# Mixer of a residual block on one core: small transfers begun a hook ahead, one attention score per step, attention's vector and scalar work at the evacuations' priority

## The chip, the cores and the metric

The kernel runs on one core of a Trainium2 chip. The metric is the device time of one execution in microseconds (us), the median of several runs. TensorE (PE) multiplies, VectorE (DVE) and ScalarE (ACT) do elementwise work, GpSimd (POOL) a little, SyncE (SP) issues the transfers.

## The reference

One layer over a sequence of 512 tokens with 2048 features: a normalised and modulated input goes through one projection, whose columns feed a gated linear recurrence (RG-LRU) and eight heads of attention with a forget gate; both are normalised, projected back and added. Then a SwiGLU feed-forward block. Cut to the part in question:

```python
mod = c_act @ w_ada[l] + b_ada[l]
sh1, sc1, gt1, sh2, sc2, gt2 = jnp.split(mod, 6, axis=-1)
h = modulate(rms_norm(x, g_mix[l]), sh1, sc1)
xr, yr, q, k, v, f_logit = jnp.split(h @ w_in[l], splits, axis=-1)
# recurrence: u = conv(xr); r, i = gates of u; a = exp(-8 r softplus(-lam))
#   h_t = a h_(t-1) + sqrt(1 - a^2) (i u);  y_rec = h * gelu(yr)
# attention, per head and block of 128 queries:
s = jnp.einsum('bhqd,bhkd->bhqk', qb, kb)
s = s + cum[:, :, q0:q1, None] - cum[:, :, None, :q1]
p = jax.nn.softmax(jnp.where(mask, s, -jnp.inf), axis=-1)
outs.append(jnp.einsum('bhqk,bhkd->bhqd', p, vb))
# x = x + gt1 * (concat(rms(y_rec), rms(y_att)) @ w_out), then the SwiGLU block
```

## The kernel before, in words

Activations lie with features on the 128 partitions and the 512 tokens along the row. Every fp32 product is three matmuls of a high and a low part (names ending in h and l), so each weight tile is transferred raw, copied to its high part by ScalarE (L187) and its low part taken by VectorE (L188). The order of the stages is: the recurrence's input columns, the first half of the gate columns, head h0, heads h1 to h7, the second half of the gate columns, then output projection, up and down projections.

A head group (`tm_group`) makes q, k and v of one head: 384 columns, 16 steps of 12 matmuls (L192), one step for each 128 input features. Work of other kinds hangs on steps as hooks: while h4's matmuls run, attention of head 3 is done, and so on. `ATT_STEPS` gives the steps after which the parts of `attention` come: statistics of q and k (L463 to L467), transposes qkt into `qkT` (L474, L476), the bias `bt` from the cumulated forget gate (L486), four scores `s` (L494) each reduced to a row minimum `nm` together with the bias (L498, in the rows CUSTOM_DVE or ISA), exponential (L500), reciprocal and scaling (L501, L502), transposes `pt` of the probabilities (L508) copied to `pT` (L511), and the products `po` with v (L519). The scores and `pt` use three PSUM buffers between them ("misc").

In h1 and h2 the sums of bias (the shift sh1 through the weights) are made: 48 transfers of 128x512 into `bw` (two buffers, L564, L565) and as many additions into `ba` (L568, L570); in h3 `binp` sums `ba` over the partitions on TensorE (L575). From h3 on, `rec_pair` does two recurrence columns per head: it loads `xrl` (L585), scales and convolves it (L587 to L592), loads gate weights `gw` (L596), makes gates on TensorE (L602) and their functions (L609 to L620, square roots L625), scans (L629) and multiplies with the gelu of `yrl` (L636 to L652). `REC_STEPS` says where its first parts stand, `CARRY` where the rest stands in the next head. Blocks of the modulation (`ada`: a transfer of 512 KB in two halves, L136, and two 128x1024 multiplications on VectorE, L139) fill up at the steps `H_ADA`.

A scheduler puts each engine's instructions into one list, by priority and by when their operands are there, and each engine runs its list in order. Evacuations of PSUM and what the next head needs stand at offset 2500 (`EVAC`), weight transfers and splits at 2000 (`AHEAD`), attention's and the recurrence's other work at the normal one, ada below it at -300 (`ADA_LATE`).

Of the kernel before, what the change touches and what calls it, by code (L numbers as in the profile page):

```python
# [44 lines left out]
YR0_AHEAD = 80  # L45
CARRY = (0, 0, 1, 1, 1, 3, 6)
WO_ADA = 5
# [15 lines left out]
def block_kernel(ctx, tc, xT, crow, adaT, vecs, bfr, w1, wyr, wqkv0, wqkv, wgate, wout, wup0, wups, wdown, outT):  # L63
# [67 lines left out]
    mods = [cp.tile([P, KT], F32, name=f"mod{j}") for j in range(6)]  # L131

    def ada_block(j, i):
        for hf in range(2):
            t = ap_.tile([P, 1024], F32, tag="ada", name=f"ada{j}_{i}_{hf}")
            nc.sync.dma_start(out=t, in_=adaT[j * KT + i, :, hf * 1024:(hf + 1) * 1024])  # L136
# [22 lines left out]

    def ada_some(n):  # L160
        with tc.high_priority(offset=ADA_LATE), tc.issue_after(tail_lo[-1]):
            for _ in range(n):
                if pending:
                    pending.pop(0)()

    def queue_ada(j, fin=None):
        for i in range(KT):
            pending.append(lambda j=j, i=i: ada_block(j, i))
        last = pending.pop()

# [240 lines left out]
    def forget(ps):  # L411
        z = cp.tile([P, NT * NH], F32, name="z")
        z3 = z.rearrange("p (t h) -> p t h", t=NT)
        for t in range(NT):
            nc.vector.tensor_add(z3[:, t, :], ps[t][:, 384:392], bfb)

        def rest():
            lf = cp.tile([P, NT * NH], F32, name="lf")
            log1p_exp(lf, z, NT * NH, "lf")
            nc.vector.scalar_tensor_tensor(out=lf, in0=z, scalar=0.0, in1=lf, op0=ALU.min, op1=ALU.subtract)  # L420
            pc = rgp("pc")
            nc.tensor.matmul(pc[:, 0:32], lhsT=triu, rhs=lf, start=True, stop=True)
# [16 lines left out]
        return rest  # L439

# [15 lines left out]
    def attention(h, q, k, v):  # L456
# [12 lines left out]
        def qk_t():  # L469
            qkT = []  # L470
            for a, z, g in ((0, q, gqs), (1, k, vcol(V_GK))):
# [3 lines left out]
                zt = page(f"qkT{h}_{a}", "b")  # L475
                nc.scalar.activation(zt, pt, AF.Copy, scale=g)  # L476
                qkT.append(zt)
# [11 lines left out]
        def score(b):  # L489
# [7 lines left out]
            nm, sm = small(1, f"nm{h}_{b}"), small(1, f"sm{h}_{b}")  # L497
            nc.vector.tensor_tensor_reduce(out=p[:, :n], in0=ps[:, :n], in1=p[:, :n], scale=-1.0, scalar=3.0e38,  # L498
                                           op0=ALU.add, op1=ALU.min, accum_out=nm)
            nc.scalar.activation(p[:, :n], p[:, :n], AF.Exp, scale=-1.0, bias=nm, accum_out=sm)  # L500
            nc.vector.reciprocal(sm, sm)  # L501
            nc.vector.tensor_scalar_mul(p[:, :n], p[:, :n], sm)  # L502

        def pt_(kb):
# [5 lines left out]
            pT = page(f"pT{h}_{kb}", "b")  # L510
            nc.scalar.activation(pT[:, qs], pt[:, qs], AF.Copy)  # L511
            st[kb] = pT
# [44 lines left out]
    ba = []  # L557

    def bias_in(kt):
        if kt == 0:  # L560
            ba.extend(page(f"ba{j}", "c") for j in range(3))
        for j, sd in enumerate((w1[kt][:, :512], w1[kt][:, 512:],
                                wyr[0][kt // 4][:, (kt % 4) * 512:(kt % 4 + 1) * 512])):
            src = ap_.tile([P, S], F32, tag="x", name=f"bw{kt}_{j}", bufs=2)  # L564
            nc.sync.dma_start(out=src, in_=sd)  # L565
            s1 = sh1[kt]
# [12 lines left out]
    def rec_pair(ns):  # L579
        X, U, GP, RG, IG, last = {}, {}, {}, {}, {}, {}  # L580
        PG = []

        def conv(n):
            x = page(f"xrl{n}", "c")
            nc.sync.dma_start(out=x, in_=xr[n])  # L585
            X[n] = x
            nc.vector.tensor_mul(x, x, rstd_x)  # L587
# [6 lines left out]
            U[n] = u  # L594
            gw = page(f"gw{n}", "c", [P, 256])
            nc.sync.dma_start(out=gw, in_=wgate[n])  # L596
            GP[n] = gw

# [23 lines left out]
        def scan():  # L622
# [5 lines left out]
            for n in ns:  # L628
                nc.vector.tensor_tensor_scan(out=U[n], data0=RG[n], data1=IG[n], initial=0.0, op0=ALU.mult, op1=ALU.add)  # L629
                hs[n] = U[n]  # L630

        def finish():
            for n in ns:
                if n < 4:
                    yl = page(f"yrl{n}", "c")
                    nc.sync.dma_start(out=yl, in_=yr[n])  # L636
                    nc.scalar.activation(yl, yl, AF.Identity, bias=bin_[:, 8 + n:9 + n])
# [31 lines left out]
    for h in range(NH):  # L669
# [413 lines left out]
```

## Time and profile before

| | |
|---|---|
| median of 3 runs | 2160.18 us (2156.42 to 2160.85) |
| the profiled execution | 2160.95 us, span 2158.9 us |
| PE busy | 2099.0 us (97%) |
| DVE busy | 1532.5 us (71%) |
| ACT busy | 859.0 us (40%) |
| mean granted clock of TensorE | 0.992 |
| the chain that ended last | PE 82%, DVE 8%, DMA 6% |

The profiled execution is 2.05 us longer than its span, the time before the first and after the last instruction. The head groups lie between 149 and 536 us; from 186 us on h1 runs. The shares above are over the whole span; the windows below split it.

### The profile page before, as it was taken

The numbers are of one execution on the slowest core, as the hardware profiler recorded it, in microseconds if no ns is written. First come the engines' busy times: TensorE is split into PE (matmuls) and PEld (weight loads), VectorE is DVE, ScalarE is ACT, GpSimd is POOL, SyncE is SP. The second block draws the span as 40 slices with busy tenths as digits, with TensorE's granted clock in tenths as the row PEclk, the third lists the DMA queues.
The fourth block names the chain that finished last, engine by engine and source line by source line (L and its number), as shares of the span: only waits on it lengthen the run. The fifth ranks groups of instructions, "written<-read, shape, count | busy, mean of one in ns | idle before, by whom it ended". The sixth has DMA issues, their size and how long they took to land.

```text
span 2158.9 us, 32248 instructions
## 1 busy us (share of the span) xinstructions
PE 2099.0 (97%) x12737; PEld 1904.1 (88%) x12737; DVE 1532.5 (71%) x2407; ACT 859.0 (40%) x1200; POOL 32.9 (2%) x37
## 2 busy tenths in 40 slices
PE   8998988989999999999999999999999999999999
PEld 6788887878878887999999999999999888888887
DVE  8997668887787689988888888888887443323332
ACT  4433336765443245544444444444444222221111
POOL 0000000000010000000000000000000000000000
PEclk9999999999999999999999999999999999999999
DMA  9987666666768742434334344344345985553442
GB/s 336 349 299 253 200 210 225 203 211 230 245 222 286 260 142 79 146 127 141 124 128 142 123 128 141 123 128 147 118 130 178 335 294 175 204 195 136 154 154 102
DMA packets 133016, 406.00 MB, mean 188 GB/s; under 512 B 14561, under 2 KB 19841, under 8 KB 123138
## 3 DMA queue, kind: packets, MB, share of 16 engines
q1 hardware_dynamic: 132866, 403.96, 55.4%
q8 instruction: 99, 1.62, 0.3%
q14 instruction: 51, 0.42, 0.1%
HBM read 361.15 MB, written 42.75 MB: 187 GB/s over the span
## 4 chain that ended last, share of the span: by engine, by line
PE 82%; DVE 8%; DMA 6%; issue 2%; ACT 1%; POOL 1%; SPq 0%; DVEq 0%; ACTq 0%
PE dn_0p L192 6%; PE dn_3p L192 6%; PE dn_2p L192 6%; PE dn_1p L192 6%; PE w1p L192 4%; PE yr1p L192 2%; PE up0p L192 2%; PE wo3p L192 2%; PE wo2p L192 2%; PE wo1p L192 2%; PE up1p L192 2%; PE yr0p L192 2%; DMA bw<-in_w 2%; DMA ada<-in_adaT 2%; PE wo0p L192 2%
## 5 line engine op out<-in xcount | busy, mean ns | idle before, releaser
L139 DVE SCALAR_TENSOR_TENSOR ada<-ada,c_b 128x1024 f32<-128x1024 f32 x128 | 154.7, 1219 | 50.0 <-DMA ada<-in_adaT 49.9
L188 DVE TENSOR_TENSOR uq_0tl<-uq_0r,uq_0th 128x1024 fp32r<-128x1024 f32 x40 | 49.0, 1225 | 62.0 <-ACT uq_0th L187 62.0
L187 ACT ACTIVATE uq_0sh<-uq_0r 128x1024 fp32r<-128x1024 f32 x40 | 42.5, 1062 | 90.6 <-PE uf6p L955 2.3
L188 DVE TENSOR_TENSOR uq_0al<-uq_0r,uq_0ah 128x1024 fp32r<-128x1024 f32 x40 | 49.0, 1225 | 39.2 <-ACT uq_0ah L187 39.1
L187 ACT ACTIVATE uq_1sh<-uq_1rb 128x1024 fp32r<-128x1024 f32 x40 | 42.5, 1063 | 70.6 <-PE uf43p L955 2.4
L187 ACT ACTIVATE uq_0th<-uq_0r 128x1024 fp32r<-128x1024 f32 x40 | 42.4, 1060 | 70.9 <-PE uf30p L955 2.1
L187 ACT ACTIVATE uq_1th<-uq_1ra 128x1024 fp32r<-128x1024 f32 x40 | 42.4, 1061 | 70.3 <-DVE uq_1sl L188 1.8
L187 ACT ACTIVATE uq_1ah<-uq_1ra 128x1024 fp32r<-128x1024 f32 x40 | 42.4, 1061 | 60.0 <-issue 58.5
L187 ACT ACTIVATE uq_0ah<-uq_0r 128x1024 fp32r<-128x1024 f32 x40 | 42.4, 1060 | 49.3 <-issue 45.5
L188 DVE TENSOR_TENSOR uq_1tl<-uq_1ra,uq_1th 128x1024 fp32r<-128x1024 f32 x40 | 49.0, 1225 | 10.0 <-ACT uq_1th L187 9.8
L570 DVE SCALAR_TENSOR_TENSOR ba<-bw,sh,ba 128x512 f32<-128x512 f32 x45 | 33.3, 749 | 27.7 <-DMA bw<-in_w 14.7
L192 PE MATMUL w1p<-hph,w1h 128*128 128x512 f32 x128 | 47.1, 396 | 6.0 <-ACT hph L333 6.0
L188 DVE TENSOR_TENSOR uq_0sl<-uq_0r,uq_0sh 128x1024 fp32r<-128x1024 f32 x40 | 49.0, 1226 | 3.7
L188 DVE TENSOR_TENSOR uq_1sl<-uq_1rb,uq_1sh 128x1024 fp32r<-128x1024 f32 x40 | 49.0, 1226 | 3.2 <-ACT uq_1sh L187 0.9
L192 PE MATMUL w1p<-hpl,w1h 128*128 128x512 f32 x128 | 50.6, 396 | 0.0
L192 PE MATMUL w1p<-hph,w1l 128*128 128x512 f32 x128 | 50.3, 393 | 0.0
L188 DVE TENSOR_TENSOR uq_1al<-uq_1ra,uq_1ah 128x1024 fp32r<-128x1024 f32 x40 | 48.6, 1214 | 0.0
L149 DVE SCALAR_TENSOR_TENSOR ada<-ada,c_b 128x1024 f32<-128x1024 f32 x32 | 38.9, 1217 | 2.4 <-DMA ada<-in_adaT 2.4
L188 DVE TENSOR_TENSOR dn_1l<-dn_2r,dn_1h 128x1024 fp32r<-128x1024 f32 x11 | 13.5, 1226 | 38.0 <-ACT dn_1h L187 38.0
L188 DVE TENSOR_TENSOR dn_0l<-dn_2r,dn_0h 128x1024 fp32r<-128x1024 f32 x11 | 13.5, 1225 | 37.6 <-ACT dn_0h L187 37.6
L188 DVE TENSOR_TENSOR dn_1l<-dn_0r,dn_1h 128x1024 fp32r<-128x1024 f32 x11 | 13.5, 1225 | 37.4 <-ACT dn_1h L187 37.4
L188 DVE TENSOR_TENSOR dn_0l<-dn_0r,dn_0h 128x1024 fp32r<-128x1024 f32 x11 | 13.5, 1226 | 37.0 <-ACT dn_0h L187 37.0
(13787 smaller groups left out, 8171.1 us busy)
## 6 DMA issues: line engine op xcount, KB each, us to landing
ada<-in_adaT SPq DMA_DIRECT2D x160, 512.0 KB, 5.5
uq_0r<-in_wups SPq DMA_DIRECT2D x80, 512.0 KB, 4.1
uq_1ra<-in_wups SPq DMA_DIRECT2D x40, 512.0 KB, 4.0
uq_1rb<-in_wups SPq DMA_DIRECT2D x40, 512.0 KB, 3.2
adf<-in_adaT SPq DMA_DIRECT2D x32, 512.0 KB, 5.9
actd<-ach SPq DMA_DIRECT2D x44, 256.0 KB, 2.0
actd<-acl SPq DMA_DIRECT2D x44, 256.0 KB, 4.0
dn_0r<-in_wdown SPq DMA_DIRECT2D x11, 1024.0 KB, 5.0
```

The source lines that it names most:

```text
L139: nc.vector.scalar_tensor_tensor(out=t, in0=t, scalar=1.0, in1=cs, op0=ALU.mult, op1=ALU.mult, accum_out=ac)
L149: nc.vector.scalar_tensor_tensor(out=t, in0=t, scalar=1.0, in1=c_b[:, cs], op0=ALU.mult, op1=ALU.mult, accum_out=ada_acc[j][:, hf, i:i + 1])
L187: nc.scalar.activation(R(hi[:, :n]), raw_ap, AF.Copy)
L188: tail_lo.append(nc.vector.tensor_sub(R(lo[:, :n]), raw_ap, hi[:, :n]).ins)
L192: nc.tensor.matmul(ps, lhsT=R(l), rhs=R(r), start=start, stop=stop)
L570: nc.vector.scalar_tensor_tensor(out=ba[j], in0=src, scalar=s1, in1=ba[j], op0=ALU.mult, op1=ALU.add)
```

## The change

It moves where parts of attention and the recurrence hang. One score comes per step (9, 10, 11, 12 in the place of two after 8 and two after 9), the first transposes of the probabilities after step 14 and their remaining parts in the next head (`TAIL_STEPS`). The recurrence's transfers get hooks of their own ahead of the work that reads them (`fetch`, `fetch_y`). The transfers into `bw` are written two ahead of their addition, those of ada one block ahead. The forget gate's end is split in two. And attention's reduction, exponential, reciprocal, scaling and the copies to `qkT` and `pT` get the priority of the evacuations.

```diff
-CARRY = (0, 0, 1, 1, 1, 3, 6)
+CARRY = (4, 4, 5, 5, 5, 7, 7, 10)
...
-    ATT_STEPS = (None, 6, 8, 8, 9, 9, 12, 12, 13, 13, 14, 14, 15, 15)
-    LAST_STEPS = (None, 3, 5, 5, 6, 6, 9, 9, 10, 10, 13, 13, 13, 13)
-    REC_STEPS = (4, 8)
+    ATT_STEPS = (None, 6, 8, 9, 10, 11, 14, 14, 15)
+    TAIL_STEPS = (0, 0, 1, 1, 2)
+    LAST_STEPS = (None, 4, 5, 6, 7, 8, 10, 10, 11, 11, 12, 12, 13, 14)
+    tail = []
+    REC_STEPS = (0, 3, 5, 9)
...
+        for n, f in zip(TAIL_STEPS, tail):
+            add(hk, n, f)
...
         if h == 0:
-            add(hk, FORGET_STEP, frest)
+            add(hk, FORGET_STEP, frest[0])
+            add(hk, FORGET_STEP + 2, frest[1])
...
+    def ada_load(j, i):
+        ts = [ap_.tile([P, 1024], F32, tag="ada", name=f"ada{j}_{i}_{hf}") for hf in range(2)]
+        for hf in range(2):
+            nc.sync.dma_start(out=ts[hf], in_=adaT[j * KT + i, :, hf * 1024:(hf + 1) * 1024])
+        ada_ready[j, i] = ts
...
-                    pending.pop(0)()
+                    pending.pop(0)[1]()
+                    if ahead and pending and pending[0][0][0] != GT2:
+                        ada_load(*pending[0][0])
...
-            nc.vector.tensor_tensor_reduce(out=p[:, :n], in0=ps[:, :n], in1=p[:, :n], scale=-1.0, scalar=3.0e38,
-                                           op0=ALU.add, op1=ALU.min, accum_out=nm)
-            nc.scalar.activation(p[:, :n], p[:, :n], AF.Exp, scale=-1.0, bias=nm, accum_out=sm)
-            nc.vector.reciprocal(sm, sm)
-            nc.vector.tensor_scalar_mul(p[:, :n], p[:, :n], sm)
+            with tc.high_priority(offset=EVAC):
+                nc.vector.tensor_tensor_reduce(out=p[:, :n], in0=ps[:, :n], in1=p[:, :n], scale=-1.0, scalar=3.0e38,
+                                               op0=ALU.add, op1=ALU.min, accum_out=nm)
+                nc.scalar.activation(p[:, :n], p[:, :n], AF.Exp, scale=-1.0, bias=nm, accum_out=sm)
+                nc.vector.reciprocal(sm, sm)
+                nc.vector.tensor_scalar_mul(p[:, :n], p[:, :n], sm)
...
+    def bias_load(n):
+        kt, j = divmod(n, 3)
+        if kt < KT:
+            sd = (w1[kt][:, :512], w1[kt][:, 512:], wyr[0][kt // 4][:, (kt % 4) * 512:(kt % 4 + 1) * 512])[j]
+            bias_src[n] = ap_.tile([P, S], F32, tag="x", name=f"bw{kt}_{j}", bufs=2)
+            nc.sync.dma_start(out=bias_src[n], in_=sd)
...
+        for j in range(3):
+            src, s1 = bias_src.pop(3 * kt + j), sh1[kt]
...
+            bias_load(3 * kt + j + 2)
...
+        def fetch(n):
+            X[n] = page(f"xrl{n}", "c")
+            nc.sync.dma_start(out=X[n], in_=xr[n])
+            GP[n] = page(f"gw{n}", "c", [P, 256])
+            nc.sync.dma_start(out=GP[n], in_=wgate[n])
...
-        return [L(conv, n0), L(conv, n1), L(gate, n0, 0), L(gate, n0, 1), L(gate, n1, 0), L(gate, n1, 1), L(gates), L(scan), L(finish)]
+        return [L(fetch, n0), L(fetch, n1), L(conv, n0), L(conv, n1), L(gate, n0, 0), L(gate, n0, 1), L(gate, n1, 0), L(gate, n1, 1), L(gates), L(scan), L(fetch_y), L(finish)]
```

What this does to the engines' lists is shown at three places, all in the attention of head 3, which runs in the steps of h4. TensorE first, before: `s_0` to `s_3` are the four scores, `pt_0` the transposes of the probabilities `bt` for the first block of keys, `po` the product with v. Where lines are left out, matmuls of h4, masks and further transposes stand.

```order
L494 MATMUL s_0_3325<-qkT_1_3277,qkT_0_3270 128x128
...
L494 MATMUL s_1_3334<-qkT_1_3277,qkT_0_3270 128x256
...
L494 MATMUL s_2_3366<-qkT_1_3277,qkT_0_3270 128x384
...
L494 MATMUL s_3_3375<-qkT_1_3277,qkT_0_3270 128x512
...
L508 MATMUL pt_0_3436<-ident,bt_0_3281 128x128
...
L192 MATMUL h4p_3076<-h_0h,hh_1562 128x384
...
L508 MATMUL pt_0_3436<-ident,bt_3_3287 128x128
...
L519 MATMUL po_3461<-pT_0_3441,v_3056 128x512
L508 MATMUL pt_2_3463<-ident,bt_2_3285 128x128
```

And TensorE after the change, at the same place:

```order
L512 MATMUL s_0_3311<-qkT_1_3253,qkT_0_3246 128x128
...
L512 MATMUL s_1_3332<-qkT_1_3253,qkT_0_3246 128x256
...
L512 MATMUL s_2_3386<-qkT_1_3253,qkT_0_3246 128x384
...
L512 MATMUL s_3_3413<-qkT_1_3253,qkT_0_3246 128x512
...
L527 MATMUL pt_0_3468<-ident,bt_0_3257 128x128
...
L204 MATMUL h4p_3061<-h_1h,hh_1646 128x384
...
L539 MATMUL po_3499<-pT_0_3473,v_3041 128x512
...
L527 MATMUL pt_2_3544<-ident,bt_2_3261 128x128
```

The scores stood in pairs with a step's 12 matmuls between the pairs; now such a step stands between each of them. `pt_0` with `bt_3` stood in the middle of the next step, now it stands with the rest of `pt_0`, and `pt_2` has moved behind the end of h4.

VectorE before, from the fourth score's reduction (the row of `s_3`) to the scaling of `bt_3`; `h_0l` is a split of a weight tile, `xrl` belongs to the recurrence:

```order
L501 RECIPROCAL sm_2_3370<-sm_2_3370 128x1
L498 ISA bt_3_3287,nm_3_3378<-s_3_3375,bt_3_3287 128x512
L498 ISA nm_3_3378 128x1
L502 TENSOR_SCALAR bt_2_3285<-bt_2_3285,sm_2_3370 128x384
L188 TENSOR_TENSOR h_0l<-h5r_3541,h_0h 128x768
L501 RECIPROCAL sm_3_3379<-sm_3_3379 128x1
L139 SCALAR_TENSOR_TENSOR ada_9_1_3492,ada_acc_115<-ada_9_1_3492,c_b 128x1024
L587 TENSOR_TENSOR xrl_3343<-xrl_3343,rstd_x 128x512
L502 TENSOR_SCALAR bt_3_3287<-bt_3_3287,sm_3_3379 128x512
```

VectorE after, the same stretch:

```order
L517 ISA bt_3_3263,nm_3_3416<-s_3_3413,bt_3_3263 128x512
L517 ISA nm_3_3416 128x1
L659 SCALAR_TENSOR_TENSOR u_2904<-g_0_3204,g_1_3206 128x512
L520 RECIPROCAL sm_2_3390<-sm_2_3390 128x1
L149 SCALAR_TENSOR_TENSOR ada_9_1_3398,ada_acc_115<-ada_9_1_3398,c_b 128x1024
L521 TENSOR_SCALAR bt_2_3261<-bt_2_3261,sm_2_3390 128x384
L520 RECIPROCAL sm_3_3417<-sm_3_3417 128x1
L200 TENSOR_TENSOR h_0l<-h5r_3526,h_0h 128x768
L521 TENSOR_SCALAR bt_3_3263<-bt_3_3263,sm_3_3417 128x512
```

The multiplication of `xrl` stood ahead of the scaling of `bt_3`; it is gone from there, a product of the recurrence (`u`) stands in the stretch instead, and one ada multiplication stands in both.

ScalarE before, around the exponentials of `bt_0` to `bt_3`; `ge` and `sqr` are the recurrence's gelu and squares:

```order
L187 ACTIVATE h_1h<-h4r_3418 128x768
L276 ACTIVATE ssq_rec<-u_2763 128x512
L544 ACTIVATE ge_3254<-ge_3254 128x512
L500 ACTIVATE bt_0_3281,sm_0_3329<-bt_0_3281,nm_0_3328 128x128
L500 ACTIVATE bt_1_3283,sm_1_3338<-bt_1_3283,nm_1_3337 128x256
L279 ACTIVATE sqr_3260<-u_2886 128x512
L500 ACTIVATE bt_2_3285,sm_2_3370<-bt_2_3285,nm_2_3369 128x384
L187 ACTIVATE h_0h<-h5r_3541 128x768
L500 ACTIVATE bt_3_3287,sm_3_3379<-bt_3_3287,nm_3_3378 128x512
```

ScalarE after:

```order
L519 ACTIVATE bt_0_3257,sm_0_3315<-bt_0_3257,nm_0_3314 128x128
L504 ACTIVATE bt_3_3263<-cb_3255,cum 128x512
L655 ACT_TABLE_LOAD
L655 ACTIVATE xrl_2668<-xrl_2668 128x512
L519 ACT_TABLE_LOAD
L519 ACTIVATE bt_1_3259,sm_1_3336<-bt_1_3259,nm_1_3335 128x256
L199 ACTIVATE h_1h<-h4r_3422 128x768
L655 ACT_TABLE_LOAD
L655 ACTIVATE xrl_2739<-xrl_2739 128x512
L519 ACT_TABLE_LOAD
L519 ACTIVATE bt_2_3261,sm_2_3390<-bt_2_3261,nm_2_3389 128x384
L519 ACTIVATE bt_3_3263,sm_3_3417<-bt_3_3263,nm_3_3416 128x512
```

Square roots of the recurrence (`xrl`) and table loads for them and for the exponential behind them stand between the exponentials now, in the place of gelu and squares. Over the whole program ScalarE has 25 table loads in its list, 19 before.

## Rows read from the trace of the kernel before

**Rows 1.** Windows, one per head: us, busy us of each engine, granted clock, DMA

```profile
338.60:392.00 53.40, 46.87 (x240) 41.82 (x239) 43.59 (x79) 36.04 (x63) 2.74 (x2) 0.94 0.59 204
392.00:438.50 46.50, 44.06 (x240) 39.78 (x239) 41.88 (x77) 35.18 (x62) 2.73 (x2) 1.00 0.70 229
438.50:489.00 50.50, 44.48 (x240) 39.72 (x239) 37.84 (x70) 31.75 (x56) 2.82 (x2) 1.00 0.61 203
489.00:535.30 46.30, 42.63 (x226) 39.02 (x225) 33.14 (x60) 26.00 (x45) 2.74 (x2) 0.96 0.65 215
```

**Rows 2.** PE's waits from 299.2 to 536: us in total, times, longest

```profile
PE pt L508 <- DVE bt L502: 14.3, 8, 4.0
PE s L494 <- DVE nm L498: 5.4, 3, 2.4
```

**Rows 3.** Windows of half clock, columns as in the first group

```profile
299.30:309.50 10.20, 10.20 (x40) 10.10 (x41) 4.38 (x7) 2.34 (x5) 0.00 (x0) 0.50 0.55 200
377.80:384.60 6.80, 5.64 (x16) 4.50 (x17) 4.50 (x8) 3.63 (x6) 0.00 (x0) 0.50 0.25 81
524.50:527.90 3.40, 3.40 (x13) 3.40 (x13) 0.91 (x1) 1.09 (x2) 0.00 (x0) 0.51 0.51 169
```

**Rows 4.** PE's waits from 186 to 299.2

```profile
PE s L494 <- DVE nm L498: 5.0, 2, 3.1
PE binp L575 <- DVE ba L570: 3.8, 1, 3.8
PE pc L422 <- DVE lf L420: 3.0, 1, 3.0
PE h3p L192 <- ACT v L453: 2.5, 1, 2.5
PE h2p L192 <- ACT v L453: 1.5, 1, 1.5
```

**Rows 5.** Chain that ended last, from 186 to 302: start us, us, what

```profile
by line: DMA bw<-in_w 34.4%; DMA bw<-in_wyr 16.6%; DVE ba L570 13.8%; DMA cb<-cum_d 4.6%; DVE h_1l L188 3.1%; DVE ss L464 3.1%; POOL ss L241 2.8%; DVE h_0l L188 2.4%; DVE qk L467 2.2%; issue 2.2%; DMA cum_d<-ct 2.1%; PE h1p L192 1.9%; PE bi
...
202.85 0.91 PE qkt L474 x8
...
291.44 6.90 DMA bw<-in_w
...
299.17 1.82 PE binp L575 x8
```

**Rows 6.** The DMA queue's own waits from 186 to 536

```profile
SPq L136 <- DVE ada L139: 78.8, 44, 4.4
SPq L565 <- DVE ba L570: 23.7, 32, 2.7
```

**Rows 7.** Timeline of PE: two neighbouring steps of head h1

```profile
192.80 0.33 PE L192 MATMUL h1p<-h_0h,hh 128*128 128x384 f32 x1
...
196.96 0.33 PE L192 MATMUL h1p<-h_1h,hh 128*128 128x384 f32 x1
```

**Rows 8.** Timeline of PE and VectorE around the longest wait for bt

```profile
364.80 1.12 PE L494 MATMUL s<-qkT,qkT 128*128 128x512 f32 x2 [2.37 <-DVE nm L498]
...
377.81 0.69 DVE L587 TENSOR_TENSOR xrl<-xrl,rstd_x 128x512 f32<-128x512 f32 x1 [3.12 <-DMA xrl<-xrd]
...
378.96 0.69 PE L508 MATMUL pt<-ident,bt 128*128 128x128 f32 x2 [3.99 <-DVE bt L502]
```

**Rows 9.** Groups by line and form, 186 to 640: busy us, mean ns

```profile
L500 ACT ACTIVATE bt<-bt,nm 128x512 f32<-128x512 f32 x8 | 5.8, 722 | 7.8 <-DVE nm L498 7.6
...
L498 DVE CUSTOM_DVE_ANT_0 bt<-s,bt 128x512 f32<-128x512 f32 x8 | 5.4, 677 | 0.0
...
L625 ACT ACT_TABLE_LOAD x4 | 5.1, 1283 | 0.1
L625 ACT ACTIVATE xrl<-xrl 128x512 f32<-128x512 f32 x8 | 5.1, 632 | 8.8 <-DVE xrl L620 8.8
...
L502 DVE TENSOR_SCALAR bt<-bt,sm 128x512 f32<-128x512 f32 x8 | 3.9, 483 | 0.1
```

More of the change, by code (lines that the diff above doesn't have):

```diff
@@ L131, in block_kernel @@
     mods = [cp.tile([P, KT], F32, name=f"mod{j}") for j in range(6)]
+    ada_ready = {}
+    def ada_load(j, i):
[3 more added lines that the diff above has]
+        ada_ready[j, i] = ts
     def ada_block(j, i):
+        if (j, i) not in ada_ready:
+            ada_load(j, i)
+        ts = ada_ready.pop((j, i))
         for hf in range(2):
-            t = ap_.tile([P, 1024], F32, tag="ada", name=f"ada{j}_{i}_{hf}")
-            nc.sync.dma_start(out=t, in_=adaT[j * KT + i, :, hf * 1024:(hf + 1) * 1024])
+            t = ts[hf]
             cs = c_b[:, hf * 1024:(hf + 1) * 1024]
@@ L158, in block_kernel, with ada_some @@
     tail_lo = []
-    def ada_some(n):
+    def ada_some(n, ahead=True):
         with tc.high_priority(offset=ADA_LATE), tc.issue_after(tail_lo[-1]):
@@ L163, in ada_some @@
                 if pending:
-                    pending.pop(0)()
+                    pending.pop(0)[1]()
+                    if ahead and pending and pending[0][0][0] != GT2:
+                        ada_load(*pending[0][0])
     def queue_ada(j, fin=None):
         for i in range(KT):
-            pending.append(lambda j=j, i=i: ada_block(j, i))
-        last = pending.pop()
+            pending.append(((j, i), lambda j=j, i=i: ada_block(j, i)))
+        at, last = pending.pop()
         def tail():
@@ L175, in tail @@
                 fin()
-        pending.append(tail)
+        pending.append((at, tail))
     def split_to(src, name, tag):
@@ L413, in forget @@
         z3 = z.rearrange("p (t h) -> p t h", t=NT)
-        for t in range(NT):
-            nc.vector.tensor_add(z3[:, t, :], ps[t][:, 384:392], bfb)
+        with tc.high_priority(offset=EVAC):
+            for t in range(NT):
+                nc.vector.tensor_add(z3[:, t, :], ps[t][:, 384:392], bfb)
+        tot = cp.tile([P, 2, 32], F32, name="tot")
         def rest():
@@ L433, in rest, with rest2 @@
                     run = tot[:, 1, t * 8:(t + 1) * 8]
+        def rest2():
+            cumf = cum.rearrange("p t h -> p (t h)")
             pt = rgp("pt")
@@ L438, in rest @@
             nc.sync.dma_start(out=cum_d, in_=ct[:32, :])
-        return rest
+        return rest, rest2
     cum_v = cum_d.rearrange("(t h) p -> h t p", h=NH)
@@ L475, in qk_t @@
                 zt = page(f"qkT{h}_{a}", "b")
-                nc.scalar.activation(zt, pt, AF.Copy, scale=g)
+                with tc.high_priority(offset=EVAC):
+                    nc.scalar.activation(zt, pt, AF.Copy, scale=g)
                 qkT.append(zt)
@@ L510, in pt_ @@
             pT = page(f"pT{h}_{kb}", "b")
-            nc.scalar.activation(pT[:, qs], pt[:, qs], AF.Copy)
+            with tc.high_priority(offset=EVAC):
+                nc.scalar.activation(pT[:, qs], pt[:, qs], AF.Copy)
             st[kb] = pT
@@ L561, in bias_in @@
             ba.extend(page(f"ba{j}", "c") for j in range(3))
[L562 to L566, printed above, removed]
+            bias_load(0)
+            bias_load(1)
+        for j in range(3):
+            src, s1 = bias_src.pop(3 * kt + j), sh1[kt]
             if kt == 0:
@@ L581, in rec_pair @@
         PG = []
+        def fetch(n):
[3 more added lines that the diff above has]
+            nc.sync.dma_start(out=GP[n], in_=wgate[n])
         def conv(n):
-            x = page(f"xrl{n}", "c")
-            nc.sync.dma_start(out=x, in_=xr[n])
-            X[n] = x
+            x = X[n]
             nc.vector.tensor_mul(x, x, rstd_x)
@@ L594, in conv @@
             U[n] = u
-            gw = page(f"gw{n}", "c", [P, 256])
-            nc.sync.dma_start(out=gw, in_=wgate[n])
-            GP[n] = gw
         def gate(n, a):
@@ L630, in scan, with fetch_y @@
                 hs[n] = U[n]
+        YL = {}
+        def fetch_y():
+            for n in ns:
+                if n < 4:
+                    YL[n] = page(f"yrl{n}", "c")
+                    nc.sync.dma_start(out=YL[n], in_=yr[n])
         def finish():
@@ L634, in finish @@
                 if n < 4:
-                    yl = page(f"yrl{n}", "c")
-                    nc.sync.dma_start(out=yl, in_=yr[n])
+                    yl = YL[n]
                     nc.scalar.activation(yl, yl, AF.Identity, bias=bin_[:, 8 + n:9 + n])
@@ L681, in block_kernel @@
         if h == 0:
-            add(hk, FORGET_STEP, frest)
-        for n, f in zip((ATT_STEPS if h < NH - 1 else LAST_STEPS)[1:], att[1:]):
+            add(hk, FORGET_STEP, frest[0])
+            add(hk, FORGET_STEP + 2, frest[1])
+        steps = ATT_STEPS if h < NH - 1 else LAST_STEPS
+        for n, f in zip(steps[1:], att[1:]):
             add(hk, n, f)
+        tail = att[len(steps):]
         if h < 2:
```

5 lines of the change are left out of this document (3 added, 2 removed).

## The prediction

> **What bounds the kernel now.** I read the page first: TensorE (PE) is busy for 97% of the span, VectorE for 71%, and the chain that ended last runs over PE for 82% of it. So only what PE waits for, and what it does at a lower clock, can be won; I then asked for PE's waits stretch by stretch and for windows by head. From 640 us on PE has no gaps that the edit could touch, and the weights streamed there are not edited. All of the change lies between 186 and 536 us, in the seven head groups h1 to h7, where attention, the recurrence and the bias sums run between the weight matmuls.
>
> There PE waits at four places. Before 299.2 us it waits for scores' reductions, for `ba` (the bias sums), for `lf` and for `v`: 5.0 + 3.8 + 3.0 + 2.5 + 1.5 = 15.8 us [rows 4]. From 299.2 to 536 it waits 14.3 us for the scaled probabilities `bt` and 5.4 us for `nm`, the reduced scores, 19.7 together [rows 2]. After longer waits the granted clock stands at 0.50 (1.2 GHz) for a while: 10.2 us behind the 3.8 us wait for `ba`, 6.8 us around the 4.0 us wait for `bt`, 3.4 us later [rows 3]. A stretch at half clock costs half its length, 5.1, 3.4 and 1.7 us.
>
> Two things stand behind these waits. Up to 299 us the chain consists for 34.4 + 16.6% of transfers into `bw` and for 13.8% of the `ba` additions [rows 5]: two buffers, each refilled only when its addition is done, one after the other until `binp`. Later it is VectorE's order. In the worst case the fourth score's matmuls begin at 364.80 and end 1.12 later; the transposes that need its result begin at 378.96, 13.0 us after, though by its durations the chain reduce, exponential, scale is 0.68 + 0.72 + 0.48 = 1.9 us [rows 8, 9]. The rest is recurrence and ada work ahead of it in VectorE's queue, 3.12 us of it a multiplication that waited for its own transfer of `xrl` [rows 8].
>
> **The change part by part.** The sum is made against the profiled execution, 2160.95 us (span 2158.9 and 2.05 outside it), which is 0.77 above the median of 2160.18.
>
> *Bias sums, up to 299 us.* The loads are written two ahead, but there are still two buffers, and the DMA queue already stands waiting for an addition to free one in 32 cases [rows 6]. So the chain of transfers keeps its pace and its end. What does move is what PE has done by then: `binp` stood after 6.17 steps of h3 and now stands after 7.33 and after the transposes qkt. A step is (196.96 − 192.80) / 2 = 2.08 us [rows 7], qkt 0.91 [rows 5]: 1.17 × 2.08 + 0.91 = 3.3 us of work moves ahead of a wait of 3.8 and fills it. The score and `lf` waits in front of it (one score per step with three score buffers, `lf` after qkt) may shrink, but what they give back is waited for at `binp` instead. Term A: −3.3. Ends: if the additions too run earlier, all the waits there can go, −15.8; if the four reductions and multiplications of one head, now at the evacuations' priority, come to stand ahead of additions, 4 × (0.68 + 0.48) = 4.6 is added, +1.3. I stay near the chain's row, since the transfers set it.
>
> *The rest of h3 and head h4's first steps.* With the wait at `binp` nearly gone, the 10.2 us of half clock behind it may go or shrink; a wait of some length will stay somewhere in front of it, so I count half of 5.1: −2.5. To it comes the part of the 19.7 us that doesn't lie in the windows of the next paragraph: those hold 53.40 − 46.87 = 6.5, 2.4, 6.0 and 3.7 us of idle PE [rows 1], 18.6, so 1.1. Term B: −3.6 (0 to −6.2).
>
> *Attention in the four heads from 338.6 to 535.3 us.* The score of step 9 no longer brings two, and the reductions, the exponential's follow-ups and the scale now go ahead of recurrence and ada on VectorE. `xrl`, the gate weights and `yrl` are loaded a hook or more ahead: they have 16 buffers, so the loads do go out earlier, and the 3.12 us wait in front of `bt` [rows 8] goes. The transposes of the first two key blocks stay three steps behind the last score (10 to 13 before, 12 to 15 now), 6.2 us, for a chain of 1.9; the rest of the transposes and the output matmuls move into the next head and have a step each. No new wait stands in front of the weight matmuls but these. What keeps this from being the full 18.6 is VectorE itself: the head from 392.0 has it busy for 41.88 of 46.5 us, 90%, and PE still idles 2.4 there at full clock [rows 1]. I take 90% as what it can be filled to. By head: the first can't go under 43.59 / 0.90 = 48.4, so 5.0 of its 6.5 + 3.4 can be won; the second stays; the third wins its 6.0 (37.84 / 0.90 = 42.0 lies far below); the fourth wins 3.7 and 1.7 of clock. Term C: −16.4. Ends: 0, if the waits merely change place, and 18.6 + 5.1 = −23.7, if nothing is left.
>
> *ScalarE.* The square roots of the recurrence now fall between the exponentials of the scores in four heads, and six more table loads stand in its program, 6 × 1.283 = 7.7 us. ScalarE is 36.04 of 53.4 us busy in its fullest head [rows 1], so the room is there; in the head shown in the change they stand in front of the second and of the third exponential, a step or two before the fourth. Counted wholly into the path from the fourth score, two loads and a square root are 2 × 1.28 + 0.63 = 3.2 [rows 9] and the chain 1.9 + 3.2 = 5.1, under the 6.2 of the three steps: nothing, as long as VectorE doesn't add over 1 us to each such chain. If it does, each us over is one of PE. The Trainium skill (page "ScalarE: Activation LUTs", section "What ACT_TABLE_LOAD costs") puts a drain of 1380 ns beside the load of 1283, 2.66 us for each switch, and its section "Table sets: the hidden batching unit" advises doing all exponentials and then all square roots, which speaks against this order. The load's 1283 ns is what the trace has; it shows no idle time of such a length behind one. By the page the chain would be 1.9 + 5.3 + 0.6 = 7.8, 1.6 us over the room, and four heads would lose 6.4 us of the gain: 2144, inside the forecast's own range below.
>
> *Ada, one block ahead, and the forget gate's tail split in two.* The DMA queue waits for an ada buffer 44 times, 78.8 us in all [rows 6]: a load written earlier has no buffer to go to. Nothing; it would cost what is queued behind it on SP, at most the longest such wait, 4.4 us. The forget part moves a wait (3.0 us for `lf`) that lies before `binp` and is inside term A.
>
> Sum: −3.3 − 3.6 − 16.4 = −23.3, which gives 2160.95 − 23.3 = 2137.7, and 2138 rounded.
>
> **The rivals.**
>
> 1. *The bias chain loosens too.* If fetches in front of it and the new order let additions follow their transfers, the waits of [rows 4] go as well: 15.8 + 19.7 of waits and 5.1 + 5.1 of clock, 45.7 us, 2115. For it: over half of the chain up to 299 us is transfers. Against it: still two buffers.
>
> 2. *The change doesn't do what it says.* The loads have no free buffers, and the gain in order is eaten by VectorE: what stood behind the scores (recurrence, ada) is now late for the next split, gate matmul or `v`, and PE waits there. Then only A stays: 2157.7, no change that a measurement of this kernel tells from none (0.2%, 4.3 us). For it: four heads with VectorE at 72 to 90%. Against it: 156.45 of 196.7 us are used, 80%, so there is slack to move work into.
>
> 3. *Slower: the fourth probability comes later than before.* Its place is the exponential, square root, exponential order on ScalarE, with VectorE's multiplications behind it. Measured once it took 13.0 us from the fourth score to the transposes [rows 8]; without the transfer's 3.1, and with the 3.2 of two loads and a square root, it is 13.1, and the room is 6.2. If all four heads behave like this one, PE waits 4 × 6.9 = 27.6 us instead of 18.6, and a wait of this length brings 6.8 us of half clock [rows 3], 3.4 us each, 13.6 in place of 5.1. With A: +9.0 + 8.5 − 3.3 = +14, some 2175. It decides from the point where the chain takes over 6.2 + 18.6 / 4 = 10.9 us. For it: the measured 13.0 and the loads. Against it: most of those 13.0 are operations that now have lower priority than the score's. By the section of the Trainium skill named above ("ScalarE: Activation LUTs", "What ACT_TABLE_LOAD costs") this chain would be 2.8 us longer still.
>
> **How the numbers follow.** Forecast 0.50, with its own range from 2129 (C and B in full) to 2148 (half of C); rival 1 0.14; rival 2 0.20; rival 3 0.16. Faster by over 0.2% holds the forecast, rival 1 and about a quarter of rival 2, whose 2157.7 lies near the bound's 2155.9: 0.69. Within 0.2%: most of the rest of rival 2, 0.15. Slower: rival 3, 0.16. The range of 8 in 10 goes from 2118, which leaves out half of rival 1, to 2162, which leaves out most of rival 3.
>
> **What would show each step.** Term A: `binp` begins within 1 us of 299, with its wait under 1 us, and the waits for scores before it are gone while the transfers into `bw` still follow each other. Term B: no half clock, or under 5 us of it, behind `binp`. Term C: waits for `bt` and `nm` together under 6 us, heads of about 46 to 48 us, VectorE at 85 to 90% in them. ScalarE: six more table loads, and no wait of PE that ends with an exponential behind one. Wrong would be the forecast if new waits of PE for `u`, for the split weights or for `v` show up with over 10 us, if `pt` waits for `bt` in every head, or if the chain of `bw` ends more than 4 us away from 299 us.

## The result, and the profile after

The changed kernel takes 2149.68 us (median of 5 runs, 2147.40 to 2152.67), the kernel before 2160.85 beside it: ratio 0.9948, interval 0.9937 to 0.9959. It is 11 us faster where 23 were forecast. The profiled execution took 2147.40 us (span 2144.3), 2.3 under its own median, 13.6 under the profiled one of before.

Where the time went is seen from the first matmul of three stages. The timeline of PE before, first rows of h4, yr1 (the second half of the gate columns) and wo1 (the second group of the output projection); the columns are start us, us, engine, line:

```profile
335.47 0.42 PE L192 MATMUL h4p<-h_0h,hh 128*128 128x384 f32 x1
...
535.11 0.48 PE L192 MATMUL yr1p<-hh,yr_0h 128*128 128x512 f32 x1
...
639.44 0.39 PE L192 MATMUL wo1p<-mx8h,wo_0h 128*128 128x512 f32 x1
```

And after:

```profile
322.85 0.74 PE L204 MATMUL h4p<-h_0h,hh 128*128 128x384 f32 x1
...
511.84 0.79 PE L204 MATMUL yr1p<-hh,yr_0h 128*128 128x512 f32 x1
...
625.36 0.39 PE L204 MATMUL wo1p<-mx8h,wo_0h 128*128 128x512 f32 x1
```

h4 begins 12.6 us earlier, yr1 23.3 earlier, wo1 only 14.1. So up to these cuts heads h1 to h3 are 12.6 shorter, h4 to h7 10.7, and yr1 with the first group of the output projection (wo0) is 9.2 longer. PE's waits after, from 186 to 299.2, which answer to [rows 4] (us in total, times, longest):

```profile
PE pc L437 <- DVE lf L435: 3.2, 1, 3.2
PE h3p L204 <- ACT v L470: 2.7, 2, 2.0
PE pt L527 <- DVE bt L521: 1.5, 1, 1.5
PE h2p L204 <- ACT v L470: 1.0, 2, 0.7
PE binp L604 <- DVE ba L598: 0.4, 1, 0.4
```

The score waits (5.0) are gone and `binp` waits 0.4 instead of 3.8. From 299.2 to 590, which answers to [rows 2]:

```profile
PE pt L527 <- DVE bt L521: 8.1, 5, 4.2
PE h7p L204 <- ACT v L470: 2.6, 2, 1.7
PE rstd_atta L265 <- DVE ssq_att L292: 1.6, 1, 1.6
PE wo0p L204 <- ACT mx12h L757: 0.7, 1, 0.7
```

The waits for `nm` are gone, those for `bt` fell from 14.3 to 8.1, and two new names stand at the end: the sum of squares of attention (`ssq_att`) and `mx12h`, a tile of the output projection. Windows of the changed kernel, h4 to h7, yr1 and wo0 (the columns of [rows 1]):

```profile
322.50:366.10 43.60, 43.60 (x240) 39.96 (x239) 36.41 (x65) 34.33 (x58) 1.83 (x2) 1.00 0.68 223
366.10:418.50 52.40, 47.20 (x240) 42.24 (x239) 44.01 (x81) 38.83 (x67) 2.20 (x2) 0.94 0.66 215
418.50:463.10 44.60, 43.73 (x239) 39.84 (x238) 36.91 (x70) 32.85 (x57) 2.52 (x2) 1.00 0.58 195
463.10:511.50 48.40, 44.35 (x240) 39.83 (x239) 38.74 (x70) 31.90 (x53) 1.83 (x2) 1.00 0.77 258
511.50:568.60 57.10, 54.78 (x250) 43.14 (x248) 38.26 (x69) 23.34 (x43) 1.83 (x2) 1.00 0.67 230
568.60:625.00 56.40, 50.80 (x216) 40.47 (x217) 46.30 (x70) 22.24 (x33) 6.83 (x7) 0.94 0.67 224
```

h4 has no idle PE at all. h5 (366.1 to 418.5) idles 5.2 us and runs part of the time at half clock (0.94). The last two answer to these windows of before:

```profile
534.80:586.70 51.90, 51.89 (x240) 41.76 (x238) 36.94 (x67) 22.30 (x40) 2.74 (x2) 1.00 0.70 243
586.70:639.10 52.40, 47.88 (x219) 38.43 (x220) 44.01 (x67) 22.50 (x33) 5.64 (x7) 1.00 0.67 225
```

yr1 took 51.9 and takes 57.1, wo0 52.4 and 56.4, at a clock of 0.94 where it was 1.00. These rows also say what the 9.2 us are. In yr1, at the same clock, PE is busy for 2.9 us more. At least 2.0 of that (run 9 below) are transposes and products of head 6 that the new steps put behind the cut: this part of the 23.3 was not won but moved. PE stands idle 2.3 us more there. In wo0 it is busy for 2.9 us more, though with three matmuls fewer, and idle 1.1 us more; the longer busy time is that of half clock, which stands in two places:

```profile
568.90:572.40 3.50, 3.50 (x9) 2.79 (x10) 3.50 (x5) 1.43 (x3) 0.00 (x0) 0.52 0.90 329
599.50:602.90 3.40, 3.17 (x8) 2.49 (x9) 3.40 (x7) 0.81 (x2) 0.00 (x0) 0.51 0.35 101
```

The first follows the wait for `ssq_att`, the second the wait for `mx0h`.

### The profile page after: what moved, and what is told of

It is laid out like the page before. It is cut to its first block, busy times and chain, and to the rows that moved or that the text cites. A ratio compares the mean times of both kernels' runs of the same rounds, so it can differ in the third digit from the quotient of the medians.

```text
span 2144.3 us, 32258 instructions
## 1 busy us (share of the span) xinstructions
PE 2096.9 (98%) x12737; PEld 1901.9 (89%) x12737; DVE 1533.0 (71%) x2407; ACT 865.3 (40%) x1206; POOL 30.1 (1%) x37
## 4 chain that ended last, share of the span: by engine, by line
PE 80%; DVE 9%; DMA 7%; ACT 2%; issue 2%; POOL 1%; SPq 0%; DVEq 0%; ACTq 0%
PE dn_0p L204 6%; PE dn_3p L204 6%; PE dn_2p L204 6%; PE dn_1p L204 6%; PE w1p L204 4%; DMA ada<-in_adaT 3%; PE up0p L204 2%; PE wo3p L204 2%; PE wo2p L204 2%; PE wo1p L204 2%; PE wo0p L204 2%; PE yr0p L204 2%; DVE ada L149 2%; DMA bw<-in_w 1%; PE h0p L204 1%
```

## The experiments

All ratios are to the kernel before, run beside each on the same chip, with 95% intervals. From the traces I also give three stretches of each profiled execution, cut at the first matmuls shown above (h1's stands between 183.2 and 185.7 us in all). With the new steps the end of a head's attention lies behind the next cut, about 2 us of PE's work; it is missing from the first column and stands in the third. From wo1 to the end all of them take 1519 to 1523 us, except run 14, which takes 1546.

| kernel | ratio | h1 to h3 | h4 to h7 | yr1 and wo0 |
|---|---|---|---|---|
| before | 1 | 151.1 | 199.6 | 104.3 |
| changed | 0.9948 (0.9937 to 0.9959) | 138.5 | 189.0 | 113.5 |
| 4: no loads ahead | 0.9949 (0.9932 to 0.9966) | 139.4 | 189.2 | 114.9 |
| 5: normal priority | 0.9991 (0.9977 to 1.0005) | 146.6 | 190.8 | 115.0 |
| 6: old attention steps | 0.9930 (0.9914 to 0.9946) | 147.9 | 184.5 | 107.7 |
| 12: before, priority only | 0.9975 (0.9961 to 0.9990) | 149.4 | 193.0 | 105.2 |
| 13: fetches only | 0.9963 (0.9950 to 0.9976) | 145.0 | 191.6 | 106.9 |
| 9: old last steps | 0.9915 (0.9894 to 0.9936) | 138.9 | 188.7 | 108.7 |
| 1: square roots early | 0.9957 (0.9940 to 0.9974) | 137.4 | 193.5 | 118.3 |
| 2: no ada transfers | 0.9868 (0.9846 to 0.9890) | 140.3 | 177.4 | 111.4 |
| 3: before, no ada transfers | 0.9916 (0.9899 to 0.9934) | 147.7 | 186.3 | 108.0 |
| 7: ada even | 0.9920 (0.9902 to 0.9938) | 142.0 | 185.4 | 110.0 |
| 8: four ada blocks | 0.9903 (0.9886 to 0.9920) | 140.6 | 180.4 | 111.7 |
| 10: 6 and 8 | 0.9904 (0.9882 to 0.9926) | 146.0 | 179.2 | 105.5 |
| 11: 9 and 8 | 0.9887 (0.9866 to 0.9908) | 140.7 | 181.3 | 106.7 |
| 14: 9, three blocks | 0.9991 (0.9982 to 1.0000) | 140.9 | 176.6 | 108.9 |

**What the parts are worth.** The loads ahead of `bw` and ada put back (4):

```diff
-                    if ahead and pending and pending[0][0][0] != GT2:
+                    if False:
...
+            bias_load(3 * kt + j)
             src, s1 = bias_src.pop(3 * kt + j), sh1[kt]
-            bias_load(3 * kt + j + 2)
```

> The changed kernel with the loads of the bias sums and of ada back at their places, the recurrence's fetches kept. My theory, two buffers leave the load ahead nowhere to go: 2148 to 2152, and the bias sums end within 1 us of where they do in the changed kernel. Rival: the bias sums ended 3 us earlier in the changed kernel because of it, 2152 to 2156.

Measured 2150.62, the same, as expected of two buffers that leave a load ahead nowhere to go. `binp` begins at 295.42 there, 1.2 us before the changed kernel's, not 3 later. The priority taken off, at all three places where the change sets it (5), and the steps put back with it on (6). These lists count steps from 0: the scores stand after 8, 9, 10 and 11 in place of two after 8 and two after 9.

```diff
-            with tc.high_priority(offset=EVAC):
+            with tc.high_priority(offset=0):
```

> The changed kernel with attention's operations back at the normal priority, everything else kept. Theory P, the priority is what shortened the waits for nm and bt: most of the gain of the heads goes, 2155 to 2161. Rival, one score per step and the moved transposes did it: 2148 to 2152. The bias sums should then end within 1 us of the changed kernel's; if they end 3 us later, it was the priority that brought them forward.

```diff
-    ATT_STEPS = (None, 6, 8, 9, 10, 11, 14, 14, 15)
+    ATT_STEPS = (None, 6, 8, 8, 9, 9, 12, 12, 13, 13, 14, 14, 15, 15)
-    LAST_STEPS = (None, 4, 5, 6, 7, 8, 10, 10, 11, 11, 12, 12, 13, 14)
+    LAST_STEPS = (None, 3, 5, 5, 6, 6, 9, 9, 10, 10, 13, 13, 13, 13)
```

> The changed kernel with the old steps of attention (two scores each after steps 8 and 9, transposes from 12 to 15, nothing in the next head), the priority and the fetches kept. Theory Q, the steps took away the waits for nm at the scores (10.4 us before, none in the changed kernel) and shortened the bias sums' way: 2154 to 2160. Rival, the priority did it: 2148 to 2152.

2157.14 and 2145.96. Without the priority the gain in the total is gone: the heads are still 13 us shorter than before, but yr1 and wo0 take 10.7 more. With the old steps the kernel is at least as fast, faster than both theories had it; theory Q is refuted as to the total, though h1 to h3 lose 9 us by it, as it said. What the two edits do before `binp` is seen in PE's waits from 186 to 299.2, of run 5 and then of run 6:

```profile
PE binp L604 <- DVE ba L598: 5.4, 1, 5.4
```

```profile
PE s L512 <- DVE nm L517: 4.0, 2, 3.5
PE binp L604 <- DVE ba L598: 4.0, 1, 4.0
```

With the new steps the score waits are gone in run 5 too, but PE then waits for `ba`, and the granted clock stands at 0.50 from 295.0 to 305.1 us behind that. The changed kernel has neither the wait nor most of the half clock. Two more runs complete the square: the priority alone on the kernel before (12), and everything but the priority and the steps (13, both edits above), which is the fetches, the loads ahead and the split forget gate.

> The kernel before with attention's operations at the evacuations' priority and nothing else. Theory P, the priority alone carries the change: 8 to 15 us under before, 2146 to 2152. Rival, it needs the recurrence's earlier transfers (the 3.1 us wait for xrl in front of bt stays in the list): within 4 us of before, 2156 to 2162.

> The changed kernel with attention's old steps and at its normal priority: what is left of the change is the recurrence's earlier transfers and their new steps, the loads ahead and the split forget gate. If the parts add in time, it is 5 to 10 us under before: the old steps with the priority were 15 us under it, the priority alone 5. If they are worth something only together with the priority (the transfer stood in front of the scaling that the priority brings forward), within 3 us of before.

2155.55 (before 2161.24), between the two expectations, and 2152.44 (before 2160.01), as expected if the parts add: the ratios are 0.9975 for the priority, 0.9963 for the earlier transfers of the recurrence with their steps, and 0.9930 for both (run 6), so these two add within their intervals. The new steps on top make it 0.9948. Without the priority the pair is 0.9991 with the new steps and 0.9963 with the old: there they cost, clear of both intervals; with it the intervals overlap.

**What was given back.** Only the last head's steps put back (9, the second pair of lines of the diff above):

> The changed kernel with only the last head's steps (LAST_STEPS) as they were. Theory T, what is given back after h7 comes from the last head's attention hanging later, so that its sum of squares is late for the output projection: the stretch from yr1's start to the end of wo0, 113.7 us in the changed kernel and 104.5 before, falls by 4 to 6, 2144 to 2146. Rival, the parts of head 6 that moved into yr1 and ada's transfers do it: under 2 us, 2148 to 2152.

2142.53 us, 0.9915: seven under the changed kernel, a little more than expected. So the last head's steps are what cost; the new steps of the other heads (run 9 against run 6, 0.9915 and 0.9930) aren't told from none. The heads are the same within 0.5 us, and yr1 with wo0 takes 108.7 in place of 113.5. What happens there is in the timelines of ScalarE and VectorE of the changed kernel, near the end of yr1 (`sqa` is the square that the sum takes in):

```profile
563.94 0.63 ACT L291 ACTIVATE sqa<-ya 128x512 f32<-128x512 f32 x1
...
565.75 1.23 DVE L149 SCALAR_TENSOR_TENSOR ada<-ada,c_b 128x1024 f32<-128x1024 f32 x1 [0.23 <-DMA ada<-in_adaT]
...
566.90 0.69 DVE L292 TENSOR_TENSOR ssq_att<-ssq_att,sqa 128x512 f32<-128x512 f32 x1
```

And of run 9:

```profile
560.18 0.64 ACT L291 ACTIVATE sqa<-ya 128x512 f32<-128x512 f32 x1
...
561.33 0.69 DVE L292 TENSOR_TENSOR ssq_att<-ssq_att,sqa 128x512 f32<-128x512 f32 x1
```

The last head's output comes later by its new steps, and its squares are done 3.8 us later (564.57 against 560.82). Then an ada multiplication that waited 0.2 us for its transfer stands in front of the sum in VectorE's list, which makes the rest of the 5.6 us: it is added at 566.90, when PE has been done with yr1 for 0.9 us, and at 561.33 in run 9, where nobody waits for it. The row of yr1 in run 9, cut at the first matmuls:

```profile
511.64:565.62 53.98, 53.90 (x249) 43.03 (x248) 38.21 (x71) 23.42 (x42) 1.83 (x2) 1.00 0.75 256
```

PE has no idle time left there, and 2.0 us more work than before (51.9). Of the two stretches of half clock in wo0 only the second is left.

**ScalarE's table loads.** The recurrence's gates and square roots three steps earlier (1), which takes every square root out from between exponentials, but moves VectorE's work on the gates too:

```diff
-CARRY = (4, 4, 5, 5, 5, 7, 7, 10)
+CARRY = (1, 1, 2, 2, 2, 4, 7, 10)
```

> The changed kernel (2149.7 us) with the recurrence's gates and square roots three steps earlier, so that no square root stands between two exponentials of the scores (19 table loads, not 25). Theory S, the interleaved square roots hold the third and fourth exponential back: the 4.2 + 0.9 us wait for bt in h5 and the half clock behind it go, 4 to 8 us less, 2142 to 2146. Rival D, VectorE's queue is late anyway: 2148 to 2152, and the wait for bt stays.

2152.84: no gain, a little above both expectations. The chain it was aimed at is long, but the loads are not what makes it so. ScalarE in h5 of the changed kernel, then PE, then the window of that stretch:

```profile
400.31 1.28 ACT L655 ACT_TABLE_LOAD   x1
401.60 0.63 ACT L655 ACTIVATE xrl<-xrl 128x512 f32<-128x512 f32 x1
...
402.99 1.28 ACT L519 ACT_TABLE_LOAD   x1
404.28 0.51 ACT L519 ACTIVATE bt<-bt,nm 128x256 f32<-128x256 f32 x1
...
409.27 0.72 ACT L519 ACTIVATE bt<-bt,nm 128x512 f32<-128x512 f32 x1 [0.42 <-DVE nm L517]
```

```profile
400.19 1.02 PE L512 MATMUL s<-qkT,qkT 128*128 128x512 f32 x2
...
411.94 0.48 PE L527 MATMUL pt<-ident,bt 128*128 128x128 f32 x1 [4.16 <-DVE bt L521]
413.27 1.11 PE L527 MATMUL pt<-ident,bt 128*128 128x128 f32 x4 [0.85 <-DVE bt L521]
```

```profile
400.00:413.00 13.00, 8.27 (x45) 7.22 (x43) 13.00 (x29) 12.47 (x20) 0.00 (x0) 0.95 0.60 186
```

The transpose at 411.94 needs the third block of `bt`, those at 413.27 the fourth. From the end of the fourth score to the latter it took 12.1 us, and PE waited 4.2 and 0.9. VectorE (the third engine of the window) is busy for all of the 13 us, so nothing that ScalarE did held it up, and the fourth exponential itself waited for VectorE's reduction `nm`. With the loads out of the way `pt` waits 7.6 us for `bt` up to yr1 (7.3 in the changed kernel, 8.1 with yr1), 3.2 of it still in h5: VectorE is late there anyway, rival D.

**Ada's transfers.** Left out from the heads to the up projection, in the changed kernel (2) and in before (3); the multiplications stay, on other data:

```diff
-        for hf in range(2):
-            nc.sync.dma_start(out=ts[hf], in_=adaT[j * KT + i, :, hf * 1024:(hf + 1) * 1024])
+        if j == GT2:
+            for hf in range(2):
+                nc.sync.dma_start(out=ts[hf], in_=adaT[j * KT + i, :, hf * 1024:(hf + 1) * 1024])
...
-            nc.vector.scalar_tensor_tensor(out=t, in0=t, scalar=1.0, in1=cs, op0=ALU.mult, op1=ALU.mult, accum_out=ac)
+            nc.vector.scalar_tensor_tensor(out=t, in0=t if j == GT2 else cs, scalar=1.0, in1=cs, op0=ALU.mult, op1=ALU.mult, accum_out=ac)
```

> The changed kernel without the transfers of ada from the heads to the up projection (the multiplications run on the vector c twice, so the modulations are wrong; same work on VectorE). Theory G, the 9 us given back after 511 us are VectorE standing in its order at ada transfers: waits for ssq_att and late starts of the output projection go, 7 to 12 us less, 2138 to 2143. Rival L, the end of the mixer is a chain of fixed length behind the second half of the gate columns: 2147 to 2152.

> The kernel before, without the same ada transfers. Theory G: before arrives later and has room for its transfers, so it wins less than the changed kernel does by the same edit, 2 to 6 us, 2155 to 2158, and the change is then worth 15 us or more. Rival L: both win the same, the change stays worth 11.

2133.73 and 2143.60. From 299.2 to 590 PE's wait for `bt` all but goes in run 2, where it was 8.1 in the changed kernel; behind it stands run 2's window from h4 to h7:

```profile
PE pt L528 <- DVE bt L522: 0.7, 1, 0.7
...
326.00:503.38 177.38, 175.76 (x955) 159.39 (x953) 156.40 (x284) 139.46 (x235) 10.21 (x8) 1.00 0.35 116
```

So ada's transfers cost 16 to 19 us, more than either theory had, but before as much as after, and the change is worth 0.9868 / 0.9916 = 0.995 without them too, as rival L had it. Theory G was right that VectorE stands at them, wrong that this is where the gain went. The two runs take the traffic away with the waits, so how much of the 16 to 19 us each of them costs is not shown. VectorE's own waits in the heads h4 to h7, before from 335 to 535, in the changed kernel from 322.5 to 511.5:

```profile
DVE ada L139 <- DMA ada<-in_adaT: 12.8, 6, 4.5
```

```profile
DVE ada L149 <- DMA ada<-in_adaT: 22.3, 16, 3.0
```

With the blocks hung evenly (7) and with four in a head and six in each output group (8):

```diff
-H_ADA = (3, 4, 7, 10, 14)
+H_ADA = (1, 4, 7, 10, 13)
```

> The changed kernel with ada's five blocks per head after steps 1, 4, 7, 10, 13 in place of 3, 4, 7, 10, 14. Theory G, VectorE stands at ada transfers because two blocks come one step apart and the third and fourth halves have no buffer yet: its wait for ada between h4 and yr1 falls from 23.8 to under 12 us, 2142 to 2147. Rival, two buffers set the pace wherever the blocks hang: 2148 to 2152.

```diff
-H_ADA = (3, 4, 7, 10, 14)
+H_ADA = (2, 6, 10, 14)
-WO_ADA = 5
+WO_ADA = 6
```

> The changed kernel with four ada blocks per head (after 2, 6, 10, 14) and six instead of five in each group of the output projection. Theory G: two waits' worth of transfers less in each head, 4 to 8 us less, 2142 to 2146. Rival, what leaves the heads is waited for in the output projection: 2148 to 2153.

2142.60 and 2139.11. Run 8 is faster than the changed kernel, by more than expected; run 7's interval touches that of the changed kernel. Evenly hung, VectorE still waits 17.1 us for them from 299.2 to 512 (23.8 in the changed kernel), not under 12, though the time is in the expected band. With four blocks (299.2 to 512, run 8) its wait falls to

```profile
DVE ada L149 <- DMA ada<-in_adaT: 4.6, 4, 2.9
```

Run 8 combined with the old steps (10), with the old last steps (11), and with three blocks in a head and eight in an output group (14, `H_ADA = (2, 7, 12)`, `WO_ADA = 8`):

> The old attention steps (as in the sixth run) and four ada blocks per head (as in the eighth) together, the priority and fetches kept. If the two gains are of different waits they add, 4 and 10 us under the changed kernel: 2134 to 2138. Rival, both relieve the same queue, VectorE's: 2138 to 2142.

> The new steps in h1 to h7, the old ones for the last head, four ada blocks per head. Theory T with G: 2133 to 2137, and the stretch from yr1 to wo0 under 108 us. Rival: as with four blocks alone, 2138 to 2141.

> As the eleventh run, with three ada blocks per head (after 2, 7, 12) and eight in each group of the output projection. If VectorE's queue at ada is still what the heads wait for, 3 to 5 us under the eleventh run. If the output projection becomes the place that waits, 0 to 6 us above it: eight blocks there are 16 transfers in 44 us, about one per 2.7 us with two buffers, and the shortest pace seen in a run of them is some 3.

2140.88, 2137.84 and 2158.76. Run 11 is the fastest kernel that does all the work, 23 us under before and ahead of the changed kernel; its interval overlaps run 8's. Runs 6 and 8 don't add, which fits the rival, that both relieve VectorE's list; no run separates that from other causes. Run 14 came out 21 us above run 11, far outside both expectations: the heads win 4.5 us over it, and the stretch from wo1 to the end loses 25. VectorE there, from 550 to 800, and then PE, from 500 to 900, where run 11 has 31.3 and 0.7 us in the first two of these rows:

```profile
DVE ada L149 <- DMA ada<-in_adaT: 39.6, 28, 4.3
```

```profile
PE rstd_1b L274 <- POOL rstd_1t L253: 11.8, 1, 11.8
PE up0p L204 <- ACT up_0h L199: 4.5, 1, 4.5
```

## Why the prediction was wrong, point by point

**The step that failed** is the sentence that all of the change lies between 186 and 536 us. At yr1's first matmul the profile has 23.3 us of gain, which is the sum of my three terms, and by luck: A and B together were too small and C too large by about the same. Then 9.2 went back. The diff changed the last head's steps and moved transposes and products of head 6 into yr1, and I priced neither. By the windows of yr1 and wo0 the 9.2 are 2.9 us of more work, at least 2.0 of it only moved, 3.4 of idle PE and 2.9 of half clock. Run 9 shows the part of the last head's steps: 4.8 of the 9.2 us in the profile, 7 in the medians; it takes the idle time out of yr1 and the half clock behind it. Of the 4.4 that stay, 2.0 are moved work. The half clock behind `mx0h` is neither: runs 6 and 13, with the old steps throughout, have a clock of 0.94 in wo0 as well. Why it is there and not in the kernel before stays open.

**Term A and B, −3.3 and −3.6, measured −12.6 together,** about 2 of it work moved into h4. The wait at `binp` fell to 0.4 as forecast and the loads ahead gave nothing that the times show (run 4). But the bias sums didn't keep their end: `binp` begins 2.6 us earlier than the 299.17 of [rows 5]:

```profile
296.57 1.05 PE L604 MATMUL binp<-ones,ba 128*128 128x1 f32 x8 [0.44 <-DVE ba L598]
```

And the score waits before it were not simply handed on to it. That takes the steps and the priority together: run 6 (old steps) and run 5 (no priority) have 147.9 and 146.6 us in this stretch, the changed kernel 138.5. In run 5 the score waits were handed on, as I had said: PE waits 5.4 us at `binp`. Of term B, the half clock behind `binp` shrank from 10.2 us to some 3.2, worth 3.5 us where I had counted 2.5:

```profile
299.20:302.40 3.20, 3.20 (x12) 3.20 (x12) 2.09 (x4) 0.84 (x1) 0.00 (x0) 0.50 0.89 304
```

**Term C, −16.4, measured −10.7.** The waits for `nm` went and h4 is without idle PE, as told. This term was mis-sized by its limit, VectorE filled to 90%, head by head. Work moved between the heads: h4 takes 43.6 us, less than the 48.4 that I had given as its floor, with VectorE busy for 36.4 and not 43.6. And in these four windows VectorE is busy for 156.1 of 189.0 us, 83%, and yet holds PE up: it stands for 22.3 us at multiplications whose transfer has not landed, with `bt` behind them in its list. 156.1 and 22.3 together are 94%. In run 2, without these transfers, it is busy for 156.4 of 177.4 us, 88%, and PE waits 0.7 us for `bt`. The term for ada, "nothing", rested on the row of the queue that issues the transfers [rows 6], which showed that loads ahead can't help (a block is two transfers of 512 KB each, for two buffers); it should have been read the other way too, that an earlier PE makes these transfers late: VectorE's wait for them grew from 12.8 to 22.3 us.

**ScalarE, nothing.** Right as far as the runs show. The chain from the fourth score to its transposes took 12.1 us in h5, over the 10.9 from which I had rival 3 decide, with 5.2 us of idle PE and a clock of 0.94; but it did so in one of four heads, and by VectorE's full list, not by the loads. So the condition that I had set for "nothing", that VectorE adds no more than 1 us to the chain, failed in that head. The Trainium skill (page "ScalarE: Activation LUTs", section "What ACT_TABLE_LOAD costs") puts a drain of 1380 ns beside the load's 1283. The rows of h5 show no drain: the next activation starts 1.29 us after the load begins. The Trainium skill advises (the same page, section "Table sets: the hidden batching unit") to do all exponentials together and then all square roots. Run 1, which does so for the scores, measures 2152.84 us, the changed kernel 2149.68: no gain here.

**The rivals.** 1 (all waits gone) did not come, 2 came in part and for the reason given, VectorE's queue: the waits for `v` at h7, 2.6 us, are new. The long chain of 3 came in h5, but not its cause, told above.

## What to carry to other kernels

Price every table that a diff edits to the end of the stage it feeds: a gain in the middle is kept only if the last consumer (here a sum of squares behind the last head) comes earlier too. An engine that runs its list in order can be full before its busy share says so (VectorE here at 83%), if operations that wait for transfers stand in front of urgent ones; count its waits into its share. And thinning the background work in such a list can be worth as much as the order of the urgent work: four blocks in a head took some 10 us off (run 8), nearly as much as the whole change. It holds as far as the next stage can take what is moved there: run 14 shows where it can't.

## What the runs showed of the hardware that I had not expected

PE's wait in wo0 for `mx2l` is 1.94 us in the changed kernel and in run 6. Here are that wait and a window behind it, of the changed kernel and then of run 6 (the clock is the third number from the end of a window):

```profile
609.80 0.50 PE L204 MATMUL wo0p<-mx2l,wo_1h 128*128 128x512 f32 x1 [1.94 <-DVE mx2l L193]
...
609.80:613.00 3.20, 3.20 (x14) 2.66 (x15) 3.20 (x6) 0.69 (x2) 0.00 (x0) 1.00 0.89 298
```

```profile
607.75 0.50 PE L204 MATMUL wo0p<-mx2l,wo_1h 128*128 128x512 f32 x1 [1.94 <-DVE mx2l L193]
...
608.50:612.00 3.50, 3.50 (x10) 2.71 (x10) 3.50 (x8) 0.00 (x0) 0.00 (x0) 0.51 0.84 331
```

Behind the wait for `mx0h` it is alike: 2.6 us before, with a clock of 1.00 through the stage, and 2.3 after, with 3.4 us of half clock. A clock loss behind a wait can't be forecast from that wait alone.
